# Attention in steps of four heads, with logits and value products in plain fp32 on halves of the array

## The chip, the core and the metric

The kernel runs on one core of a Trainium2 chip. The metric is the device time of one execution in microseconds (us). The engines are PE (TensorE, matmuls; PEld is its weight load), DVE (VectorE), ACT (ScalarE), POOL (GpSimd) and SP, which issues most DMAs.

## The reference

One layer of a decoder trunk on 256 positions of 1024 channels. Three attention branches stand beside each other: MoBA attention (A, 4 heads; with 256 positions one block, so plain causal attention with a position bias), forgetting attention (B, 4 heads, the bias is a running sum of log gates) and sliding-window attention with sinks (C, 8 query heads over 2 key heads). Heads have 64 channels. All is float32.

```python
z = rmsnorm(x, ln1) @ w_in            # q, k, v of A, B, C; forget gates; three merge gates
o_a = moba_attention(qa, ka, va, tbl_a)
o_b = forgetting_attention(qb, kb, vb, fb + b_f)
o_c = sliding_window_sink_attention(qc, kc, vc, sinks, tbl_c)
#   each: softmax(q k^T * SCALE + bias, causal or windowed) v
merged = sigmoid(ga) * (o_a @ w_pa) + sigmoid(gb) * (o_b @ w_pb) + sigmoid(gc) * (o_c @ w_pc)
x = x + merged @ w_o
u = causal_dwconv(rmsnorm(x, ln2) @ w_up, conv_w, conv_b)
a, b = split(u)
out = rmsnorm(x + (silu(a) * b) @ w_down, ln_f)
```

## The kernel before

All large products use fp32r, a one-pass format, three times: an operand is split into a high part (a copy by ACT into an fp32r tile, `hi`) and a low part (a subtraction by DVE, `lo`), and TensorE adds high x high, low x high and high x low (`mm3`, lines 254 to 258). The weights stream in by DMA as `raw` pieces of 128x1024; ACT makes `whi` of each (line 110) and DVE `wlo` (line 117), up to five pieces ahead of their matmuls.

The order of all instructions is written out by hand. A generator, `filler`, yields the projection matmuls one by one, each with an estimate of its time: q and k of B, v of B, q and k of A, v of A and C, q of C, k of C (line 407 and `mm3`), then six gate groups of 48 matmuls with 512 columns (`group_gates`). `now` is the sum of these estimates. Everything else is a task, a generator that does one stage, then yields a delay after which its next stage is put between the filler's matmuls. `AT` has the starting times of the tasks and `DL` the delays. Engines run their own instructions in the order written, so a stage that is not ready holds up what stands behind it.

Attention is eight tasks, `pair(p)`, p from 0 to 7, of two heads each: 0 and 1 are B, 2 and 3 are A, 4 to 7 are C. The two heads of a pair are in partitions 0 to 63 and 64 to 127 of q. The keys are stored twice, each with the other head's half set to zero by POOL, so that one matmul over all 128 rows gives both heads' logits side by side. Stages of a pair:

- logits (line 610): for each half of the 256 queries three fp32r matmuls, of 256 columns (keys 0 to 127 of both heads) into bank `s0` and of 512 (all keys) into `s1`;
- softmax: DVE adds the bias and takes the minimum of the negated logits (line 618), ACT takes the exponential and the sums (line 627), DVE scales by the reciprocal (line 640);
- six 128x128 transposes of the weights into banks `pt` and `o` (line 647), copied out by ACT, with a low part by DVE (lines 650 to 654);
- values (lines 660 and 663): six fp32r matmuls of 256 columns with zero-padded v, and two plain fp32 ones of 128 columns for the second half of the keys, into `pt`;
- the result's high and low part (lines 666 and 668) in `oT`, which the output projections read later.

PSUM has eight banks: four `acc` for the projections, and `s0`, `s1`, `pt`, `o` with one buffer each, so a new use of one of them waits until the last reader of the earlier one is done. Behind attention come the output projections, the merge, and the MLP, which the change doesn't touch.

Of the kernel before, what the change touches and what calls it, by code (L numbers as in the profile page):

```python
# [35 lines left out]
AT = dict(norm=1.59, positions=9.23, out0=26.0, out1=20.0, gates=18.2, sums=23.0, pairs=(37.46,  # L36
          44.7, 52.4, 61.33, 67.8, 74.76, 83.2, 90.9), mm=14.0)
DL = dict(pos=1.0, sq0=0.5, sq1=0.53, rs=1.0, row=1.0, q=1.98, qlo=1.17, v=0.83, vlo=0.8, g1=0.47,
          g2=0.64, s1=1.0, s2=1.43, s3=1.0, b=0.8, qk=1.9, ex=2.56, sc=1.21, fl=0.45, fl2=0.71,
          lo=0.8, va=0.91, vh=0.6)  # L40
# [100 lines left out]
def hybrid_kernel(ctx: ExitStack, tc: tile.TileContext, x, xT, ln_f, w_main, w_v1, w_v2, b_f, sinks,  # L141
# [88 lines left out]
    def q_tiles(n, name):  # L230
        return [at.tile([P, n, S], F32R, name=name + x) for x in "hl"]

    def k_tiles(n, name):

        ks = [at.tile([P, n, 2, S], F32R, name=name + x) for x in "hl"]
        for k in ks:
            nc.gpsimd.memset(k[0:64, :, 1, :].bitcast(F32), 0.0)
            nc.gpsimd.memset(k[64:128, :, 0, :].bitcast(F32), 0.0)
        return ks

    def v_tiles(n, name):

        vs = [at.tile([P, n, 2, P], F32 if x == "1" else F32R, name=name + x) for x in "hl1"]
        for v in vs:
            w = v if v is vs[2] else v.bitcast(F32)
            nc.gpsimd.memset(w[:, :, 0, 64:128], 0.0)
            nc.gpsimd.memset(w[:, :, 1, 0:64], 0.0)
        return vs

    qB, qA, qC = q_tiles(2, "qB"), q_tiles(2, "qA"), q_tiles(4, "qC")  # L250
    kB, vB, kA, vA = k_tiles(2, "kB"), v_tiles(2, "vB"), k_tiles(2, "kA"), v_tiles(2, "vA")
    kC, vC = k_tiles(1, "kC"), v_tiles(1, "vC")
# [172 lines left out]
    room = G[:, 0].rearrange("p t (n c) -> p (t n) c", c=512)  # L425
    turn = [0]

    def scaled(acc, width, scale):

        turn[0] += 1  # L430
        tmp = room[:, turn[0] % 4, :width].rearrange("p (b s) -> p b s", s=S)
        r = rs["row1"][:, None, :].to_broadcast([P, width // S, S])
        nc.vector.scalar_tensor_tensor(tmp, acc[:, :width].rearrange("p (b s) -> p b s", s=S),
                                       scale, r, op0=OP.mult, op1=OP.mult)
        return tmp

    def q_out(dst, b0, acc):
        bs = slice(b0, b0 + 2)
        tmp = scaled(acc, 512, SCALE)
        nc.scalar.activation(dst[0][:, bs], tmp, AF.Copy)  # L440
        return lambda: nc.vector.tensor_sub(dst[1][:, bs], tmp, dst[0][:, bs].bitcast(F32))

    def k_out(dst, acc, width):
        tmp = scaled(acc, width, 1.0)
        halves = list(enumerate((slice(0, 64), slice(64, 128))))
        for e, h in halves:
            nc.scalar.activation(dst[0][h, :, e, :], tmp[h], AF.Copy)

        def low():
            for e, h in halves:  # L450
                nc.vector.tensor_sub(dst[1][h, :, e, :], tmp[h], dst[0][h, :, e, :].bitcast(F32))
        return low

    def v_out(dst, acc, t):
        a = acc.rearrange("p (b e d) -> p b e d", e=2, d=HD)
        r = rs[1][:, t:t + 1]
        hs = [dst[2 if t else 0][:, :, e, e * 64:e * 64 + 64] for e in range(2)]
        for e in range(2):
            nc.scalar.activation(hs[e], a[:, :, e, :], AF.Identity, scale=r)

        def low():
            for e in range(2):
                lo = dst[1][:, :, e, e * 64:e * 64 + 64]
                nc.vector.scalar_tensor_tensor(lo, a[:, :, e, :], r, hs[e].bitcast(F32),
                                               op0=OP.mult, op1=OP.subtract)
        return low if t == 0 else None

    def group_qk(q, k, name, later=None):
        accs = [bank("acc", 512, 4) if later is None else bank(tag, 512) for tag in ("pt", "o")]
        for i in range(4):  # L470
            yield from qk_piece(accs, 2 * i, 2, 512)

        def out():
            assert "row1" in done
            low = q_out(q, 0, accs[0])
            yield DL["q"]
            low2 = q_out(q, 2, accs[1]) if k is None else k_out(k, accs[1], 512)
            low()
            yield DL["qlo"]
            low2()  # L480
            done.add(name)
        spawn(out(), 0.0 if later is None else later)

    def group_kc():
        acc = bank("acc", 512, 4)
        yield from qk_piece([acc], 0, 8, P)

        def out():
            low = k_out(kC, acc, S)
            yield DL["qlo"]  # L490
            low()
            done.add("kC")
        spawn(out())
# [3 lines left out]
    def group_v1():  # L497
# [9 lines left out]
        def out():  # L507
            low = v_out(vB, accs[0][:, 0:256], 0)
            v_out(vB, accs[1][:, 0:256], 1)
            yield DL["v"]  # L510
            low()
            done.add("vB")
        spawn(fox(logits), AT["gates"])
        spawn(out(), AT["out1"])

    def group_v2():
# [4 lines left out]
        def out():  # L521
            low = [v_out(vA, accs[0][:, 0:256], 0), v_out(vC, accs[0][:, 256:384], 0)]
            yield DL["v"]
            v_out(vA, accs[1][:, 0:256], 1)
            v_out(vC, accs[1][:, 256:384], 1)
            for f in low:
                f()
            done.add("vA")
        spawn(out())
# [74 lines left out]
    def pair(p):  # L604
        q, qi, k, ki, v, vi, bias, j = pair_of(p)
        assert done >= ({"B", "vB", "foxb"} if p < 2 else {"A", "vA"} if p < 4 else {"C", "kC"}), p
        s0, s1 = bank("s0", S), bank("s1", 512)
        for sc, qs, n in ((s0, slice(0, P), P), (s1, slice(P, S), S)):
            for i, (a, b) in enumerate(((0, 0), (1, 0), (0, 1))):
                nc.tensor.matmul(sc, q[a][:, qi, qs], k[b][:, ki, :, 0:n], start=i == 0,  # L610
                                 stop=i == 2)
        yield DL["qk"]
        L = at.tile([P, 2, ROWS], F32, name="L", tag="L", bufs=1)
        nm = small([2, 2], "nm")
        for e in range(2):
            least = 3.0e38 if j is None else skn[:, j + 4 * e:j + 4 * e + 1]
            for i, (sc, lo, n) in enumerate(((s0, 0, P), (s1, P, S))):
                nc.vector.tensor_tensor_reduce(
                    out=L[:, e, lo:lo + n], in0=sc[:, e * n:(e + 1) * n], in1=bias[e][i],
                    scale=-1.0, scalar=least, op0=OP.add, op1=OP.min, accum_out=nm[:, e, i:i + 1])  # L620
        sm, sd = small([2, 2], "sm"), small([2, 2], "sd")
        if j is not None:
            nc.vector.tensor_sub(sd, nm, skn[:, j:j + 5:4][:, :, None].to_broadcast([P, 2, 2]))
        for e in range(2):
            for i, (lo, n) in enumerate(((0, P), (P, S))):
                a = L[:, e, lo:lo + n]
                nc.scalar.activation(a, a, AF.Exp, scale=-1.0, bias=nm[:, e, i:i + 1],
                                     accum_out=sm[:, e, i:i + 1])
        if j is not None:
            nc.scalar.activation(sd, sd, AF.Exp)  # L630
        done.add(p)
        yield DL["ex"]
        if j is not None:
            nc.vector.tensor_add(sm, sm, sd)
        r = small([2, 2], "rs")
        nc.vector.reciprocal(r, sm)
        for e in range(2):
            for i, (lo, n) in enumerate(((0, P), (P, S))):
                a = L[:, e, lo:lo + n]
                nc.vector.tensor_scalar(a, a, r[:, e, i:i + 1], None, op0=OP.mult)  # L640
        yield DL["sc"]
        pTh, pTl, pT1 = [at.tile([P, 2, n], d, name="pT" + x, tag="pT" + x, bufs=1)
                         for x, n, d in (("h", S, F32R), ("l", S, F32R), ("1", P, F32))]
        pts = [bank(tag, ROWS) for tag in ("pt", "o")]
        for e in range(2):
            for i in range(3):
                nc.tensor.transpose(pts[e][:, i * P:(i + 1) * P], L[:, e, i * P:(i + 1) * P], ident)  # L647
            yield DL["fl"] if e else DL["fl2"]
        for e in range(2):
            nc.scalar.activation(pTh[:, e, :], pts[e][:, 0:S], AF.Copy)  # L650
            nc.scalar.activation(pT1[:, e, :], pts[e][:, S:ROWS], AF.Copy)
        yield DL["lo"]
        for e in range(2):
            nc.vector.tensor_sub(pTl[:, e, :], pts[e][:, 0:S], pTh[:, e, :].bitcast(F32))
# [431 lines left out]
```

## Time and profile before

| | |
|---|---|
| median of 3 runs | 392.74 us (392.5 to 393.16) |
| the profiled execution | 392.43 us, span of its instructions 390.7 us |
| busy: PE, DVE, ACT, POOL | 97%, 77%, 61%, 4% of the span |
| PE's granted clock | 0.996 on the mean of the span |

A matmul's record is longer than the time that it adds, since matmuls are pipelined; the chain of work that ended last shows the time that each adds. A plain fp32 matmul leaves two records, an fp32r matmul or a transpose one. A form such as 34*12 behind a name is the part of the array that a matmul uses, rows by columns.

### The profile page before, as it was taken

The page shows a single profiled execution, that of the slowest core. Times are in us where ns is not written, and L with a number is a line of the kernel's source. Part 1 is how long each engine was busy: PE and PEld are TensorE (multiplying, and loading weights), DVE is VectorE, ACT ScalarE, POOL GpSimd, SP SyncE. Part 2 cuts the span into 40 slices and gives each one's busy share as a digit, 9 for nine tenths or more (in the row PEclk, how much of TensorE's full clock was granted, in tenths as well). Part 3 has the DMA queues.
Part 4 walks back from the last instruction along what each step waited for, and adds up shares of the span by engine and source line. Part 5 has one row for each costly group of instructions (what it writes and reads, how often), then busy time and mean ns, then how long its engine had stood idle before and what let it go on. Part 6 is the DMA issues. An engine that isn't in the chain of part 4 may idle for free.

```text
span 390.7 us, 6636 instructions
## 1 busy us (share of the span) xinstructions
PE 379.8 (97%) x2464; PEld 345.7 (88%) x2464; DVE 301.6 (77%) x572; ACT 239.5 (61%) x431; POOL 15.7 (4%) x50
## 2 busy tenths in 40 slices
PE   5999999999999999999999999999999999999992
PEld 5999999888888888888899999999999999999982
DVE  3877998775876727967779999878887888888745
ACT  4875767647566587326587767655665556655533
POOL 4711000000000000000000000000000000000000
PEclk9999999999999999999999999999999999999998
DMA  7989775442533446443736567656465655463002
GB/s 188 393 315 331 281 213 179 153 132 103 187 125 117 164 141 235 161 163 107 269 109 216 168 227 251 209 182 204 164 208 180 206 167 201 173 216 108 2 1 108
DMA packets 21376, 70.88 MB, mean 181 GB/s; under 512 B 2504, under 2 KB 3413, under 8 KB 21344
## 3 DMA queue, kind: packets, MB, share of 16 engines
q1 hardware_dynamic: 20448, 68.05, 51.8%
q0 software_dynamic: 752, 2.18, 1.8%
q8 instruction: 19, 0.31, 0.3%
q10 hardware_dynamic: 144, 0.23, 0.2%
q14 instruction: 13, 0.11, 0.1%
HBM read 69.38 MB, written 1.07 MB: 180 GB/s over the span
## 4 chain that ended last, share of the span: by engine, by line
PE 96%; DMA 1%; DVE 1%; SPq 0%; ACT 0%; issue 0%; DVEq 0%
PE s L874 16%; PE acc L256 15%; PE acc L258 15%; PE acc L257 15%; PE pt L874 8%; PE o L874 8%; PE acc L407 7%; PE s L610 2%; PE pt L660 1%; DMA raw<-in_w_main 1%; PE pt L407 1%; PE o L407 1%; PE pt L663 1%; PE o L647 1%; PE pt L647 1%; PE s L314 0%
## 5 line engine op out<-in xcount | busy, mean ns | idle before, releaser
L117 DVE TENSOR_TENSOR wlo<-raw,whi 128x1024 fp32r<-128x1024 f32 (+4 forms) x131 | 150.5, 1162 | 15.4 <-ACT whi L110 15.2
L110 ACT ACTIVATE whi<-raw 128x1024 fp32r<-128x1024 f32 (+4 forms) x131 | 129.0, 1006 | 34.9 <-PE acc L257 21.0
L256 PE MATMUL acc<-whi,hThi 128*128 128x512 f32 (+2 forms) x160 | 62.3, 390 | 0.0
L258 PE MATMUL acc<-wlo,hThi 128*128 128x512 f32 (+2 forms) x160 | 60.1, 376 | 0.0
L257 PE MATMUL acc<-whi,hTlo 128*128 128x512 f32 (+2 forms) x160 | 59.9, 374 | 0.0
L874 PE MATMUL s<-oThi,whi 128*128 128x256 f32 x176 | 49.3, 281 | 0.0
L874 PE MATMUL s<-oThi,wlo 128*128 128x256 f32 x176 | 49.2, 280 | 0.0
L874 PE MATMUL s<-oTlo,whi 128*128 128x256 f32 x176 | 48.9, 280 | 0.0
L882 ACT ACTIVATE ya<-v,cv 128x256 f32<-128x256 f32 x22 | 13.3, 603 | 42.7 <-DVE v L879 42.7
L258 PEld LDWEIGHTS acc<-wlo,hThi 128*128 128x128 f32 x160 | 30.0, 188 | 5.3
L257 PEld LDWEIGHTS acc<-whi,hTlo 128*128 128x128 f32 x160 | 30.2, 189 | 4.5 <-DVE hTlo L308 0.2
L256 PEld LDWEIGHTS acc<-whi,hThi 128*128 128x128 f32 x160 | 30.1, 188 | 4.3
L257 PE MATMUL acc<-whi,al 128*128 128x512 f32 (+1 forms) x88 | 33.8, 384 | 0.0
L258 PE MATMUL acc<-wlo,ah 128*128 128x512 f32 (+1 forms) x88 | 33.8, 384 | 0.0
L256 PE MATMUL acc<-whi,ah 128*128 128x512 f32 (+1 forms) x88 | 33.8, 384 | 0.0
L874 PEld LDWEIGHTS s<-oTlo,whi 128*128 128x128 f32 x176 | 33.5, 191 | 0.0
L874 PEld LDWEIGHTS s<-oThi,whi 128*128 128x128 f32 x176 | 33.0, 188 | 0.4
L874 PEld LDWEIGHTS s<-oThi,wlo 128*128 128x128 f32 x176 | 33.0, 188 | 0.4
L874 PE MATMUL pt<-oThi,whi 128*128 128x256 f32 x88 | 24.8, 282 | 0.0
L874 PE MATMUL pt<-oThi,wlo 128*128 128x256 f32 x88 | 24.7, 281 | 0.0
L874 PE MATMUL pt<-oTlo,whi 128*128 128x256 f32 x88 | 24.7, 281 | 0.0
L874 PE MATMUL o<-oThi,whi 128*128 128x256 f32 x88 | 24.7, 281 | 0.0
(301 smaller groups left out, 802.1 us busy)
## 6 DMA issues: line engine op xcount, KB each, us to landing
raw<-in_w_main SPq DMA_DIRECT2D x115, 512.0 KB, 3.3
raw<-in_w_main SPq DMA_DIRECT2D x7, 256.0 KB, 5.9
raw<-in_w_v SPq DMA_DIRECT2D x4, 384.0 KB, 4.2
xt<-in_x SPq DMA_DIRECT2D x2, 512.0 KB, 6.9
G<-rowsd POOLq DMA_DIRECT2D x1, 1024.0 KB, 13.7
raw<-in_w_v SPq DMA_DIRECT2D x2, 390.0 KB, 6.3
G<-in_xT SPq DMA_DIRECT2D x3, 256.0 KB, 6.3
out_y<-xt SPq DMA_DIRECT2D x2, 288.0 KB, 2.2
```

The source lines that it names most:

```text
L110: self.nc.scalar.activation(self.parts[i][0][:, cs], self.raw[i][:, cs], AF.Copy)
L117: self.nc.vector.tensor_sub(lo[:, cs], self.raw[i][:, cs], hi[:, cs].bitcast(F32))
L256: nc.tensor.matmul(o, lh, rh, start=start, stop=False, **kw)
L257: nc.tensor.matmul(o, ll, rh, start=False, stop=False, **kw)
L258: nc.tensor.matmul(o, lh, rl, start=False, stop=stop, **kw)
L407: nc.tensor.matmul(o, w[:, kk, cs], hT[h][:, k, :], start=first, stop=last, skip_group_check=True)
L610: nc.tensor.matmul(sc, q[a][:, qi, qs], k[b][:, ki, :, 0:n], start=i == 0, stop=i == 2)
L647: nc.tensor.transpose(pts[e][:, i * P:(i + 1) * P], L[:, e, i * P:(i + 1) * P], ident)
L660: nc.tensor.matmul(o, v[a][:, vi, e, :], b[:, e, :], start=e == 0 and n == 0, stop=False, **kw)
L663: nc.tensor.matmul(o[:, P:S], v[2][:, vi, e, :], pT1[:, e, :], start=False, stop=e == 1, **kw)
L874: nc.tensor.matmul(u, w, h2T[h][:, k, :], start=k == 0 and i == 0, stop=k == KD - 1 and i == 2)
L882: nc.scalar.activation(y, v, AF.Identity, scale=w[2], bias=w[3])
```

## The change

`four(n)`, n from 0 to 3, takes the place of `pair(p)` and handles pairs 2n and 2n+1 in each stage. q, k and v are kept in float32 as they come, with no high and low part, no second copy and no zeros; ACT or DVE writes each once. The logits of a head are plain fp32 matmuls on its 64 partitions, so each head of a pair uses its own half of the array's rows; they go into one bank per head. The values of a head are plain fp32 matmuls with 64 columns of v as weights, each head of a pair in its own half of the array's columns, into the two halves of one bank. The transposed weights are copied out once, in float32. The tables of times and delays are new.

```diff
-          s3=1.0, b=0.8, qk=1.9, ...
+AT = dict(norm=1.59, positions=9.23, out0=26.0, out1=20.0, gates=18.2, sums=23.0,
+          fours=(37.46, 53.0, 68.5, 83.5), mm=14.0)
+DL = dict(pos=1.0, sq0=0.5, sq1=0.53, rs=1.0, row=1.0, q=1.98, g1=0.47, g2=0.64, s1=1.0, s2=1.43,
+          s3=1.0, b=0.8, qk=1.9, half=2.0, ex=2.6, sc=1.3, fl=1.2, va=1.9, vh=0.9)
...
+    def qk_tiles(n, name):
+        return at.tile([P, n, S], F32, name=name)
     def v_tiles(n, name):
+        return [at.tile([P, n, 2, HD], F32, name=name + x) for x in "01"]
...
+    def scaled(dst, acc, scale):
+        n = dst.shape[1]
+        r = rs["row1"][:, None, :].to_broadcast([P, n, S])
+        nc.vector.scalar_tensor_tensor(dst, acc[:, :n * S].rearrange("p (b s) -> p b s", s=S),
                                        scale, r, op0=OP.mult, op1=OP.mult)
...
     def v_out(dst, acc, t):
         a = acc.rearrange("p (b e d) -> p b e d", e=2, d=HD)
         r = rs[1][:, t:t + 1]
+        nc.scalar.activation(dst[t], a, AF.Identity, scale=r)
...
+    def four(n):
+        need = ({"B", "vB", "foxb"}, {"A", "vA"}, {"C", "kC"}, {"C", "kC"})[n]
+        assert done >= need, n
+        pairs = [pair_of(2 * n + i) for i in range(2)]
+        sc = [bank(tag, ROWS) for tag in ("s0", "s1", "pt", "o")]
+        for i, (q, qi, k, ki, *_) in enumerate(pairs):
+            for lo, qs, m in ((0, slice(0, P), P), (P, slice(P, S), S)):
+                for e in range(2):
+                    h = slice(e * HD, (e + 1) * HD)
+                    nc.tensor.matmul(sc[2 * i + e][:, lo:lo + m], q[h, qi, qs], k[h, ki, 0:m],
+                                     start=True, stop=True)
         yield DL["qk"]
...
+            yield DL["ex"] if i else DL["half"]
...
+        pT = at.tile([P, 4, ROWS], F32, name="pT", tag="pT", bufs=1)
+        pts = [bank(tag, ROWS) for tag in ("s0", "s1", "pt", "o")]
+        for h in range(4):
             for i in range(3):
+                nc.tensor.transpose(pts[h][:, i * P:(i + 1) * P], L[:, h, i * P:(i + 1) * P], ident)
+        yield DL["fl"]
+        for h in range(4):
+            nc.scalar.activation(pT[:, h, :], pts[h], AF.Copy)
         yield DL["va"]
         kw = dict(skip_group_check=True)
+        os = [bank(tag, S) for tag in ("s0", "s1")]
+        for i, (*_, v, vi, _, _) in enumerate(pairs):
+            for t, cs in ((0, slice(0, S)), (1, slice(P, S))):
+                for e in range(2):
+                    p = pT[:, 2 * i + e]
+                    nc.tensor.matmul(os[i][e * HD:(e + 1) * HD, cs], v[t][:, vi, e, :],
+                                     p[:, S:ROWS] if t else p[:, 0:S], start=t == 0, stop=t == 1,
+                                     **kw)
         yield DL["vh"]
+        for i in range(2):
+            nc.scalar.activation(oT[0][:, 2 * n + i, :], os[i], AF.Copy)
         yield DL["vh"]
+        for i in range(2):
+            nc.vector.tensor_sub(oT[1][:, 2 * n + i, :], os[i],
+                                 oT[0][:, 2 * n + i, :].bitcast(F32))
```

The order on TensorE at the first logits. Before, pair 0 has six fp32r matmuls over the whole array (`kBh`, `kBl`, `qBh`, `qBl` are the high and low parts):

```order
L610 MATMUL s_791<-kBh,qBh 128x256 [waits DVE_49,Activation_49,Pool_49]
L610 MATMUL s_791<-kBh,qBl 128x256
L610 MATMUL s_791<-kBl,qBh 128x256 [waits Pool_49]
L610 MATMUL s_792<-kBh,qBh 128x512 [waits DVE_49]
L610 MATMUL s_792<-kBh,qBl 128x512
L610 MATMUL s_792<-kBl,qBh 128x512
```

Now, at the same place, the first step has eight matmuls, the two heads of a pair in turn (s0 and pt are the heads on rows 0 to 63, s1 and o those on rows 64 to 127):

```order
L566 MATMUL s0_728<-kB_143,qB_140 128x128 [waits DVE_49]
L566 MATMUL s1_729<-kB_143,qB_140 128x128 [waits DVE_49]
L566 MATMUL s0_728<-kB_143,qB_140 128x256
L566 MATMUL s1_729<-kB_143,qB_140 128x256
L566 MATMUL pt_730<-kB_143,qB_140 128x128
L566 MATMUL o_731<-kB_143,qB_140 128x128
L566 MATMUL pt_730<-kB_143,qB_140 128x256
L566 MATMUL o_731<-kB_143,qB_140 128x256
```

All four heads of B now have their logits here; before, pair 1 followed 72 matmuls later.

The order on TensorE around the values of A's last heads. Before, three gate matmuls out of nine that follow are shown, and the wait of what comes next is one for the softmax's result:

```order
L660 MATMUL pt<-pTl,vAh 128x256
L660 MATMUL pt<-pTl,vAh 128x256 [waits DVE_49]
L663 MATMUL pt<-pT_1248,vA_169 128x128
L663 MATMUL pt<-pT_1248,vA_169 128x128 [waits Activation_49]
L256 MATMUL acc<-whi,hThi 128x512
L257 MATMUL acc<-whi,hTlo 128x512
L258 MATMUL acc<-wlo,hThi 128x512
```

Now the values of the second step are followed by three gate matmuls and then by the logits of the third:

```order
L619 MATMUL s_1133<-pT,vA_148 64x256 [waits PE_49,Activation_49]
L619 MATMUL s_1133<-pT,vA_148 64x256 [waits Activation_49]
L619 MATMUL s_1133<-pT,vA_149 64x128 x2
L243 MATMUL acc<-whi,hThi 128x512
L244 MATMUL acc<-whi,hTlo 128x512
L245 MATMUL acc<-wlo,hThi 128x512
L566 MATMUL s_1155<-kC,qC 128x128 [waits DVE_49]
L566 MATMUL s_1156<-kC,qC 128x128 [waits DVE_49]
L566 MATMUL s_1155<-kC,qC 128x256
L566 MATMUL s_1156<-kC,qC 128x256
```

The logits moved up to the values whose two banks they use again: they wait for DVE's subtractions of these values.

On DVE at the same place, now (`G<-acc` is the eviction of the second gate group, `oTlo` the low part of the values):

```order
L646 TENSOR_SCALAR G<-acc,nq 128x512 [waits PE_49]
L116 TENSOR_TENSOR wlo<-raw,whi 128x1024 [waits DMAHW5_49,Activation_49]
L627 TENSOR_TENSOR oTlo<-s_1132,oThi 128x256 [waits Activation_49]
L627 TENSOR_TENSOR oTlo<-s_1133,oThi 128x256 [waits Activation_49]
L578 ISA L,nm<-s_1155,G,skn 128x128 [waits DVE_49,DMASW7_49,PE_49,Pool_49]
```

The two subtractions stand behind an eviction and a weight remainder; before, a single one stood at a pair's end and freed `pt` alone.

In the last two steps the logits of the fourth stand directly ahead of the values of the third, which take banks s0 and s1 next:

```order
L566 MATMUL pt<-kC,qC 128x256
L566 MATMUL o<-kC,qC 128x256
L619 MATMUL s_1344<-pT,vC_150 64x256 [waits DVE_49]
L619 MATMUL s_1344<-pT,vC_150 64x256
L619 MATMUL s_1344<-pT,vC_151 64x128 x2
```

Before, no pair's logits stood directly ahead of another's values: at least 6 projection matmuls lay between them.

## Rows read from the trace of the kernel before

**Rows 1.** The page: span, TensorE's busy time, granted clock, chain that ended last.

```profile
span 390.7 us, 6636 instructions
...
PE 379.8 (97%) x2464; PEld 345.7 (88%) x2464; DVE 301.6 (77%) x572; ACT 239.5 (61%) x431; POOL 15.7 (4%) x50
...
PEclk9999999999999999999999999999999999999998
...
PE 96%; DMA 1%; DVE 1%; SPq 0%; ACT 0%; issue 0%; DVEq 0%
```

**Rows 2.** Busy time by stretch: length, then engines, granted clock, DMA share, GB/s.

```profile
50.00:150.00 100.00, 100.00 (x563) 86.50 (x562) 70.89 (x181) 66.97 (x156) 0.56 (x1) 1.00 0.46 150
```

**Rows 3.** Chain of work, pair 0 and pair 1: start, time on the path, what.

```profile
51.76 0.12 PE acc L407
51.88 1.06 PE s L610 x6
...
59.41 0.33 PE pt L647 x3
...
60.57 0.33 PE o L647 x3
...
61.50 1.05 PE s L610 x6
...
64.58 0.72 PE pt L660 x6
65.30 0.45 PE pt L663 x4
```

**Rows 4.** Chain of work around the 34-row matmul, line 381.

```profile
17.48 0.72 PE o L407 x6
18.20 0.74 PE s L381 x2
18.94 0.91 PE pt L407 x6
```

**Rows 5.** Chain of work around the four 8-row matmuls, line 576.

```profile
40.85 0.17 PE acc L257
...
41.20 0.65 PE s L576 x4
41.85 0.37 PE acc L256
```

**Rows 6.** Chain of work around the two transposes into 8 partitions, line 568.

```profile
38.19 0.22 PE s L568 x2
38.41 0.71 PE acc L407 x6
```

**Rows 7.** Chain of work: plain fp32, two of 128 columns; one of 4.

```profile
24.50 0.45 PE s L302 x4
...
34.76 0.22 PE s L557 x2
```

**Rows 8.** Lines by form, ACT and DVE, 50 to 150 us: busy us, mean ns.

```profile
L110 ACT ACTIVATE whi<-raw 128x1024 fp32r<-128x1024 f32 x28 | 29.4, 1058 | 14.8 <-PE acc L257 12.3 <-issue 1.1 <-ACT kCh L447 0.8
L666 ACT ACTIVATE oThi<-pt 128x256 fp32r<-128x256 f32 x8 | 3.0, 381 | 3.7 <-PE pt L663 3.7
...
L117 DVE TENSOR_TENSOR wlo<-raw,whi 128x1024 fp32r<-128x1024 f32 x30 | 36.2, 1220 | 8.9 <-ACT whi L110 8.8
L668 DVE TENSOR_TENSOR oTlo<-pt,oThi 128x256 fp32r<-128x256 f32 x8 | 3.4, 423 | 7.2 <-ACT oThi L666 7.2
L686 DVE TENSOR_SCALAR G<-acc,nq 128x512 f32<-128x512 f32 x4 | 3.0, 752 | 6.4 <-PE acc L258 6.4
```

**Rows 9.** Timeline of DVE: the reductions of two heads of C.

```profile
96.92 0.35 DVE L618 CUSTOM_DVE_ANT_0 L<-s,G,skn 128x128 f32<-128x128 f32 x1 [0.29 <-issue]
...
97.60 0.35 DVE L618 CUSTOM_DVE_ANT_0 L<-s,G,skn 128x128 f32<-128x128 f32 x1
```

**Rows 10.** Timeline of PE: start, length. Then the chain's time for 512 columns.

```profile
56.85 0.28 PE L407 MATMUL acc<-hTlo,whi 128*128 128x256 f32 x1
...
56.97 0.28 PE L407 MATMUL acc<-hThi,wlo 128*128 128x256 f32 x1
...
101.61 0.23 PE acc L257
```

More of the change, by code (lines that the diff above doesn't have):

```diff
@@ L228, in hybrid_kernel @@
     at = attn_ctx.enter_context(tc.tile_pool(name="attn", bufs=1))
[L230 to L239, printed above, removed]
-    def v_tiles(n, name):
[L243 to L252, printed above, removed]
+    def qk_tiles(n, name):
+        return at.tile([P, n, S], F32, name=name)
+    def v_tiles(n, name):
+        return [at.tile([P, n, 2, HD], F32, name=name + x) for x in "01"]
+    qB, qA, qC = qk_tiles(2, "qB"), qk_tiles(2, "qA"), qk_tiles(4, "qC")
+    kB, kA, kC = qk_tiles(2, "kB"), qk_tiles(2, "kA"), qk_tiles(1, "kC")
+    vB, vA, vC = v_tiles(2, "vB"), v_tiles(2, "vA"), v_tiles(1, "vC")
     def mm3(o, lhs, rhs, start, stop, **kw):
@@ L474, in out @@
             assert "row1" in done
-            low = q_out(q, 0, accs[0])
+            scaled(q[:, 0:2], accs[0], SCALE)
             yield DL["q"]
[L477 to L480, printed above, removed]
+            if k is None:
+                scaled(q[:, 2:4], accs[1], SCALE)
+            else:
+                scaled(k, accs[1], 1.0)
             done.add(name)
@@ L507, in out @@
         def out():
[L508 to L511, printed above, removed]
+            for t in range(2):
+                v_out(vB, accs[t][:, 0:256], t)
             done.add("vB")
+            yield 0.0
         spawn(fox(logits), AT["gates"])
@@ L521, in out @@
         def out():
[L522 to L527, printed above, removed]
+            for t in range(2):
+                v_out(vA, accs[t][:, 0:256], t)
+                v_out(vC, accs[t][:, 256:384], t)
             done.add("vA")
+            yield 0.0
         spawn(out())
@@ L602, in pair_of @@
         return qC, j, kC, 0, vC, 0, bias, j
[L604 to L611, printed above, removed]
-        yield DL["qk"]
[L613 to L645, printed above, removed]
-            for i in range(3):
[L647 to L654, printed above, removed]
@@ new lines, in four @@
+    def four(n):
[9 more added lines that the diff above has]
+                                     start=True, stop=True)
+        yield DL["qk"]
+        L = at.tile([P, 4, ROWS], F32, name="L", tag="L", bufs=1)
+        nm, sm, sd, r = (small([4, 2], x) for x in ("nm", "sm", "sd", "rs"))
+        for i in range(2):
+            bias, j = pairs[i][6:]
+            hs = slice(2 * i, 2 * i + 2)
+            for e in range(2):
+                least = 3.0e38 if j is None else skn[:, j + 4 * e:j + 4 * e + 1]
+                h = 2 * i + e
+                for t, (lo, m) in enumerate(((0, P), (P, S))):
+                    nc.vector.tensor_tensor_reduce(
+                        out=L[:, h, lo:lo + m], in0=sc[h][:, lo:lo + m], in1=bias[e][t],
+                        scale=-1.0, scalar=least, op0=OP.add, op1=OP.min,
+                        accum_out=nm[:, h, t:t + 1])
+            if j is not None:
+                nc.vector.tensor_sub(sd[:, hs], nm[:, hs],
+                                     skn[:, j:j + 5:4][:, :, None].to_broadcast([P, 2, 2]))
+            for h in (2 * i, 2 * i + 1):
+                for t, (lo, m) in enumerate(((0, P), (P, S))):
+                    a = L[:, h, lo:lo + m]
+                    nc.scalar.activation(a, a, AF.Exp, scale=-1.0, bias=nm[:, h, t:t + 1],
+                                         accum_out=sm[:, h, t:t + 1])
+            if j is not None:
+                nc.scalar.activation(sd[:, hs], sd[:, hs], AF.Exp)
+            yield DL["ex"] if i else DL["half"]
+        done.update((2 * n, 2 * n + 1))
+        for i in range(2):
+            hs = slice(2 * i, 2 * i + 2)
+            if pairs[i][7] is not None:
+                nc.vector.tensor_add(sm[:, hs], sm[:, hs], sd[:, hs])
+            nc.vector.reciprocal(r[:, hs], sm[:, hs])
+            for h in (2 * i, 2 * i + 1):
+                for t, (lo, m) in enumerate(((0, P), (P, S))):
+                    a = L[:, h, lo:lo + m]
+                    nc.vector.tensor_scalar(a, a, r[:, h, t:t + 1], None, op0=OP.mult)
+            yield DL["sc"]
+        pT = at.tile([P, 4, ROWS], F32, name="pT", tag="pT", bufs=1)
+        pts = [bank(tag, ROWS) for tag in ("s0", "s1", "pt", "o")]
+        for h in range(4):
+            for i in range(3):
+                nc.tensor.transpose(pts[h][:, i * P:(i + 1) * P], L[:, h, i * P:(i + 1) * P], ident)
+        yield DL["fl"]
+        for h in range(4):
+            nc.scalar.activation(pT[:, h, :], pts[h], AF.Copy)
@@ L655, in pair @@
         yield DL["va"]
-        o = bank("pt", S)
         kw = dict(skip_group_check=True)
-        for n, (a, b) in enumerate(((0, pTh), (1, pTh), (0, pTl))):
-            for e in range(2):
-                nc.tensor.matmul(o, v[a][:, vi, e, :], b[:, e, :], start=e == 0 and n == 0,
-                                 stop=False, **kw)
-        for e in range(2):
-            nc.tensor.matmul(o[:, P:S], v[2][:, vi, e, :], pT1[:, e, :], start=False, stop=e == 1,
-                             **kw)
+        os = [bank(tag, S) for tag in ("s0", "s1")]
@@ L667, in pair @@
         yield DL["vh"]
-        nc.vector.tensor_sub(oT[1][:, p, :], o, oT[0][:, p, :].bitcast(F32))
+        for i in range(2):
+            nc.vector.tensor_sub(oT[1][:, 2 * n + i, :], os[i],
+                                 oT[0][:, 2 * n + i, :].bitcast(F32))
     def group_gates(br, half):
@@ L717, in hybrid_kernel @@
     spawn(positions(), AT["positions"])
-    for p, u in enumerate(AT["pairs"]):
-        spawn(pair(p), u)
+    for n, u in enumerate(AT["fours"]):
+        spawn(four(n), u)
     for cost in filler():
```

44 lines of the change are left out of this document (4 added, 40 removed).

## The prediction

> **What bounds the kernel now.** I read the page first. TensorE is busy for 97% of the 390.7 us span at the full granted clock (2.4 GHz), and the chain that ended last is 96% PE [rows 1]. Attention runs between 50 and 150 us, so the stretch is what matters: there PE is busy 100 of 100 us, DVE 70.89, ACT 66.97, and DMA at 0.46 [rows 2]. Busy TensorE alone proves little, since a matmul's record is 0.28 us long while the next starts 0.12 us later [rows 10]. So I read the chain of work in order of time, which gives each matmul's own share of the path: pieces follow each other without a gap, 0.12 us for a 256-column and 0.23 us for a 512-column fp32r matmul [rows 3, 10]. Nothing on DVE, ACT or POOL ends a wait of TensorE here. What counts is the number of TensorE slots in the eight pairs, and any wait that the new order puts between them.
>
> **What a pair costs on TensorE.** Logits: six fp32r matmuls, 1.05 us. Transposes: twice three, 0.33 us each time, 0.11 us apiece. Values: six fp32r matmuls, 0.71 us, and two plain fp32 ones (four records), 0.45 us [rows 3]. Two pairs, which is one of the new steps of four heads: logits 2.10, transposes 1.32, values 2.32 us. There are four such steps.
>
> **What leaves at no gain.** The low parts of q, k, v and of the transposed softmax weights, and the zero halves, are work of DVE, ACT and POOL, and none of it ends a TensorE wait; it lies under a TensorE that is busy throughout [rows 2]. Costed at nothing; the cover is the gate matmuls, and nothing is exposed by taking covered work away. Transposes are unchanged in number: nothing.
>
> **What TensorE does instead.** Per step of four heads, the logits are eight plain fp32 matmuls on half the rows (four of 128 columns, four of 256), the values eight on half the columns, of the same sizes. A plain fp32 matmul has two records, and of 128 columns it takes half of 0.45 us: 0.11 us a record, call it u [rows 7]. The 384-column one bears this out as linear: 0.74 us, of which 0.10 is the switch below, is 0.64, or six records' worth of u [rows 4]. So a 256-column one is 4u, a 128-column one 2u.
> - One after another, a block of eight is 4 x 2u + 4 x 4u = 24u = 2.64 us. That is the upper bound; all rows of plain fp32 here are of this kind.
> - If the two heads of a pair run fully beside each other, it is 12u = 1.32 us, the lower bound.
> - In between: matmuls start in the order written, and each has two records on its own half. First head first record, first head second record, second head first record: the third may run beside the second, but not beside the first. Laying out the sixteen records so (each starts when its half is free and the one before it has started), both blocks end at 15u = 1.65 us. No row shows two halves at once. I take this value since the rows show an array that takes the next matmul long before the last one has left (0.12 against 0.28 us [rows 10]), and two halves share neither rows nor, in the logits, a bank.
> - Weight loads: three fp32 matmuls with 4 columns still take about 0.11 us a record [rows 7], so a full-width load alone holds the path for u. The logits block has 16 of these loads; if they queue, it takes 16u = 1.76 us rather than 1.65. The values' loads are half as wide and fit. I take 1.76 and 1.65.
>
> **Switching the array's division.** The kernel before already does this three times. Around the four matmuls on 8 rows: they take 0.65 where four take 0.48 (+0.17), and the first 384-column matmul after them takes 0.37 instead of 0.17 (+0.20), so in and out cost 0.37 [rows 5]. Around the 34-row matmul: 0.10 going in and 0.91 instead of 0.72 for the six after it, 0.29 together [rows 4]. But the two transposes into 8 output partitions, a split by columns alone, take 0.22 for two and 0.71 for the six after: no cost [rows 6]. So a logits block (split by rows) pays 0.37; a values block (by columns) pays between 0 and 0.37, and I take 0.20. The Trainium skill (TensorEngine Tiling (Array Packing), Key Properties) says that a change of tiling mode, not just of tile, drains TensorE, which speaks against this change; rows 4 and 5 agree, rows 6 do not show it. By that rule every block pays 0.37, and the sum would be 4 x 0.17 = 0.7 us higher. In the last two steps the logits of one stand directly ahead of the values of the other, which saves one switch, 0.2 us in all.
>
> **The waits that the new order adds.** Banks s0, s1, pt and o now serve logits, transposes and values in turn, so a step can block the next.
> - At the end of the second gate group (call it time 0) the order is: values of the second step, three gate matmuls, logits of the third, which wait for the values' banks. TensorE gets there at 1.85 + 0.70 = 2.55 us. ACT has a weight conversion first (1.06), then the two copies of the values (0.38 each): done near 1.5 and 1.9. DVE has the gate group's eviction (0.75) and a weight remainder (1.22) first, until 2.1, then the two subtractions (0.42 each): 2.5 and 2.9 [rows 8]. The second logits matmul needs s1 at about 2.65: some 0.3 us of wait, with all later gate matmuls queued behind it.
> - The values of the third step stand right behind the logits of the fourth and need s0 and s1 back from DVE's reductions, two for a head in 0.68 us (from 96.92 to 97.60 [rows 9]). The first head's logits end about 1.1 us into the block, so s0 is free near 1.9, when TensorE is done with the logits (1.96): at most 0.1 us.
> - Transposes come 85 small or 54 large matmuls after their logits (10 us or more), and values 15 large ones (3.5 us) after the transposes, against four copies of some 0.5 us and a conversion (1.06): no wait, with about 0.4 us to spare. If ACT is late by more than that, this is the next wait.
> Together 0.4 us; the ends are 0 and about 3.
>
> **The sum.** Per step: logits 1.76 + 0.37 - 2.10 = +0.03; values 1.65 + 0.20 - 2.32 = -0.47. Four steps: -1.76. Shared switch -0.2, waits +0.4: **-1.55 us**. The profiled execution took 392.43 us (span 390.7, 1.73 around it), 0.31 below the median of the runs shown, 392.74; I put the difference on the median: **391.2 us**. With the column switch at its ends (-0.8 to +0.7) and the waits from 0 to 1.4, this case alone gives 390.0 to 392.9.
>
> **The rivals.**
> - *No overlap.* Each half waits for the other, 24u a block: logits +0.91, values 2.64 + 0.20 - 2.32 = +0.52, four times 1.43 = 5.7, less 0.2, plus 0.4: +5.9, **398.6 us**. For it: every fp32 row here is serial, and 256 columns of plain fp32 are 0.44 us against 0.12 of one fp32r pass, so without overlap two heads cost more than three padded passes. Against it: only the depth of the pipeline. It decides as soon as a block takes more than about 20u: then logits and values together lose what they now gain.
> - *Full overlap.* 12u a block, loads too: logits -0.41, values -0.80, four times -1.21 = -4.84, less 0.2, plus 0.8 since DVE then returns the banks later than TensorE wants them: -4.2, **388.5 us**. Nothing in the trace decides it; against it speaks that each matmul's two records follow each other on one half. The Trainium skill (TensorE: Matmul & The Clock Gate, Part 3) has matmuls in different tiles start about 4 ns apart and run concurrently; by that rule this is the case that comes, and no row here shows it.
> - *One split overlaps, the other not.* Logits alone: (0.03 + 0.52) x 4 + 0.2 = +2.4; values alone: (0.91 - 0.47) x 4 + 0.2 = +2.0. About **394.9 us**. The two splits are different: by rows two banks are written, by columns one bank, and both heads then read all 128 rows.
> - *The banks come back late.* If DVE or ACT is one more weight conversion behind at two or three of the places above, the waits are 3 us instead of 0.4: **393.8 us**. It decides from 2 us of waits on. For it: four tasks now share four banks; against it: DVE and ACT have 30 us of every 100 free [rows 2] and lose work.
>
> **Chances.** Forecast 0.38, full overlap 0.18, no overlap 0.27, one split only 0.12, late banks 0.05. A measurement of this kernel can tell about 0.2%, 0.8 us. The forecast's own range (390.0 to 392.9) lies seven parts in ten below 391.95, the rest within; full overlap is faster; the other three are slower. Faster 0.45, same 0.11, slower 0.44. Both signs hold much, so the range must reach from full overlap into the case without it: 388.4 to 399.0; less than 2 in 10 lies outside.
>
> **What would show it.** In the chain of work after: logits blocks of 8 matmuls near 1.8 us (1.3 with full overlap, 2.6 without), values blocks near 1.65; 0.2 us extra on the first matmul behind each; TensorE idle or stretched by 0.3 us ahead of the third step's logits; all else as before, DVE and ACT less busy. The forecast is wrong if a block takes 20u or more, or if a TensorE wait for DVE or ACT of over 1 us stands before a logits or values block.

## The result, and the profile after

The changed kernel takes **387.99 us** (median of 4 runs, 387.09 to 388.68). The kernel before took 392.95 us beside it (392.5 to 393.94, 4 runs). The ratio is 0.9875, with a 95% interval of 0.9857 to 0.9893: 1.25% or 5.0 us faster. 391.2 us was forecast: the direction was right, the gain was three times as large, and the time is what the rival *full overlap* gave (388.5).

The page of the changed kernel, the lines that answer to [rows 1]:

```profile
span 387.0 us, 6530 instructions
...
PE 377.2 (97%) x2464; PEld 340.1 (88%) x2464; DVE 287.7 (74%) x540; ACT 230.7 (60%) x399; POOL 8.0 (2%) x20
...
PEclk9899999999999999999999999999999999999998
...
PE 96%; DMA 1%; DVE 1%; SPq 0%; ACT 0%; issue 0%; DVEq 0%
```

Its busy time by stretch, the columns as in [rows 2]:

```profile
50.00:150.00 100.00, 99.81 (x588) 82.62 (x587) 61.62 (x156) 65.23 (x139) 0.56 (x1) 1.00 0.47 156
5.00:10.00 5.00, 3.03 (x17) 2.62 (x17) 2.09 (x6) 2.63 (x6) 0.37 (x1) 0.95 0.98 276
10.00:15.00 5.00, 5.00 (x33) 5.00 (x33) 4.77 (x11) 4.28 (x9) 0.58 (x1) 0.71 1.05 407
```

TensorE still bounds attention. DVE has lost 9 of 71 us there and ACT 2 of 67, and TensorE now stands still for 0.2 us. The two lower lines are the start-up of this one execution: the granted clock is 0.71 on the mean of 10 to 15 us, a mix of the two levels 1.2 and 2.4 GHz, after a stretch in which TensorE was busy 3.03 of 5 us (the profiled execution before was busy 2.41 there and kept 1.00). Some executions of nearly every kernel here have a lower mean clock and take some 1.3 us longer, so medians hold a mix, and differences below 1 us are read from the traces.

The chain of work, first and second step, answers to [rows 3] (start, time on the path, what; L566 logits, L619 values, L394 and L243 projections):

```profile
53.12 0.86 PE s L566 x8
53.98 0.10 PE pt L566
54.08 0.01 PE o L566
...
54.62 0.01 PE o L566
```

```profile
70.36 1.45 PE s L619 x16
71.81 0.43 PE acc L243
```

The logits block is done at 54.63: 1.51 us for four heads, where two pairs took 2.10 before. The values block takes 1.45, where two pairs took 2.32. The first matmul behind a block takes 0.43 where the next ones take 0.23, so leaving the halves costs 0.20. With u = 0.109 us (a record of 128 columns of plain fp32, the prediction's 0.11) 12u is 1.31: the logits block is 12u and 0.20 for the switch, the values block 12u and 0.14.

The timeline of TensorE in the second half of that logits block (start, length; `pt` is the head on rows 0 to 63, `o` that on rows 64 to 127) shows where the time went:

```profile
53.81 0.27 PE L566 MATMUL pt<-kB,qB 64*128 64x128 f32 x1
53.82 0.27 PE L566 MATMUL o<-kB,qB 64*128 64x128 f32 x1
53.92 0.27 PE L566 MATMUL pt<-kB,qB 64*128 64x128 f32 x1
53.93 0.27 PE L566 MATMUL o<-kB,qB 64*128 64x128 f32 x1
```

Each head's records of 128 columns follow each other at u, and those of the other head start 0.01 us behind. The Trainium skill (TensorE: Matmul & The Clock Gate, Part 3) has matmuls in different tiles start about 4 ns apart; this trace agrees, with 0.01 us.

The chain at the third step's logits, and where the fourth's logits meet the third's values:

```profile
95.81 1.00 PE s L566 x5
...
97.25 0.43 PE o L566 x2
97.68 0.43 PE acc L243
```

```profile
114.88 0.91 PE s L566 x8
115.79 0.33 DVE L L578
...
116.13 0.40 DVE L L578
...
116.59 1.55 PE s L619 x16
118.14 0.43 PE acc L243
```

The third block takes 1.87 instead of 1.51: 0.36 us for bank `s1`, which DVE's subtraction returns late. At the fourth, logits and values begin 1.71 us apart, 0.2 of which is a wait for DVE's reductions, and the values take 1.55, 0.10 more than where they follow without a wait: 0.30 in all. These are the only two waits of TensorE, 0.66 us together.

The bookkeeping of attention, in the two profiled executions: before, from the first logits at 51.88 to the end of the last values at 143.58, 91.70 us; after, 53.12 to 136.81, 83.69 us. 15 gate matmuls fewer lie between (3.45 us), so attention itself saves 4.56. The blocks give 4 x (1.51 + 0.20 - 2.10) + 4 x (1.45 + 0.20 - 2.32) = -4.24, the shared switch -0.2, the waits +0.66: -3.8. The other 0.8 lie in the projection matmuls between; there are 11 interruptions now and 32 before. By the starts of their records, gate matmuls follow each other at 0.227 us where nothing has come between for long, and some 0.005 wider in the first ten behind an interruption; from 75 us on this adds up to 0.5 us before and 0.15 now. It accounts for about half of the 0.8; the rest stays open.

### The profile page after: what moved, and what is told of

Read it like the earlier page. It is cut to its first block, busy times and chain, and to the rows that moved or that the text cites. A ratio compares the mean times of both kernels' runs of the same rounds, so it can differ in the third digit from the quotient of the medians.

```text
span 387.0 us, 6530 instructions
## 1 busy us (share of the span) xinstructions
PE 377.2 (97%) x2464; PEld 340.1 (88%) x2464; DVE 287.7 (74%) x540; ACT 230.7 (60%) x399; POOL 8.0 (2%) x20
## 4 chain that ended last, share of the span: by engine, by line
PE 96%; DMA 1%; DVE 1%; SPq 0%; ACT 0%; issue 0%; DVEq 0%
PE s L834 16%; PE acc L243 16%; PE acc L244 15%; PE acc L245 15%; PE pt L834 8%; PE o L834 8%; PE acc L394 7%; PE pt L394 2%; PE s L619 2%; PE o L394 1%; DMA raw<-in_w_main 1%; PE s L566 1%; PE s L608 1%; PE s L301 0%; PE pt L566 0%; PE pt L773 0%
## 5 line engine op out<-in xcount | busy, mean ns | idle before, releaser
L243 PE MATMUL acc<-whi,hThi 128*128 128x512 f32 (+2 forms) x160 | 61.3, 383 | 0.0
L243 PEld LDWEIGHTS acc<-whi,hThi 128*128 128x128 f32 x160 | 30.1, 188 | 6.0 <-issue 1.3
L243 PE MATMUL acc<-whi,ah 128*128 128x512 f32 (+1 forms) x88 | 33.8, 384 | 0.0
```

The source lines that it names most:

```text
L243: nc.tensor.matmul(o, lh, rh, start=start, stop=False, **kw)
```

## The experiments

After the result this was to be told apart: whether the halves overlap wherever their matmuls stand, or only where neighbours in the order are on different halves; what the steps of four heads are worth beside the halves; and whether the relief of DVE, ACT and POOL has a share in the gain.

**Halves apart.** All matmuls of one half first, then those of the other, in the logits:

```diff
-        for i, (q, qi, k, ki, *_) in enumerate(pairs):
-            for lo, qs, m in ((0, slice(0, P), P), (P, slice(P, S), S)):
-                for e in range(2):
+        for e in range(2):
+            for i, (q, qi, k, ki, *_) in enumerate(pairs):
+                for lo, qs, m in ((0, slice(0, P), P), (P, slice(P, S), S)):
```

> The changed kernel with the logits of a step written head by head over both pairs: all four matmuls on rows 0 to 63 first, then all four on rows 64 to 127. Same work, same switches. Theory (the two halves run beside each other because matmuls of the two heads stand next to each other in the order written): a logits block grows from 12 to about 24 units of 0.11 us, from 1.5 to 2.8 us in the chain, four times 1.3 = 5.3 us more: about 393.3 us. Rival 1 (the array takes any matmul whose half is free, in whatever order): no change, 388.0. Rival 2 (the gain of the change does not come from halves at all but from less work on DVE, ACT and POOL): no change either.

389.88 us (389.46 to 391.59), ratio 0.9928 [0.9904, 0.9952]. Neither number came. The chain of work at the first block:

```profile
51.51 0.85 PE s L566 x4
...
53.12 0.66 PE o L566 x4
53.78 0.43 PE acc L394 x2
```

and its timeline where the second half begins (`pt` is the fifth record of the first half, `s` is bank `s1`, the first record of the second; PEld is its weight load):

```profile
52.20 0.27 PE L566 MATMUL pt<-kB,qB 64*128 64x128 f32 x1
52.20 0.18 PEld L566 LDWEIGHTS s<-kB,qB 64*128 64x128 f32 x1
52.20 0.37 PE L566 MATMUL s<-kB,qB 64*128 64x128 f32 x1
52.31 0.27 PE L566 MATMUL pt<-kB,qB 64*128 64x128 f32 x1
...
52.42 0.27 PE L566 MATMUL s<-kB,qB 64*128 64x128 f32 x1
```

2.27 us: 0.20 and 19u, where wholly one after another would be 24u. The second half starts 7u after the first, while its own first matmul stands eight records behind; three records ahead of it in the order start later than it does. So a half is not bound to the order written, but it does not see past every matmul ahead of it. Four blocks longer by 0.76 are 3.0 us, and the two waits (0.66) have gone: +2.4. Attention (51.51 to 137.62) is 86.11 us against 83.69, +2.4. At the fourth step no wait stands between logits and values any more, and the values are back at 1.45:

```profile
116.84 0.66 PE o L566 x4
117.50 1.45 PE s L619 x16
```

The same edit in the values:

> The changed kernel with the values of a step written head by head: all four matmuls on columns 0 to 63 first, then all four on columns 64 to 127. Theory: a values block grows from 1.45 to about 2.8 us in the chain, four times 1.3 = 5.3 us more: about 393.3 us. Rivals as for the logits: no change, 388.0. If only one of the two splits overlaps by neighbourhood, this and the run with the logits apart differ.

390.83 us (389.54 to 391.6), ratio 0.9946 [0.9921, 0.9972]. The chain of work has the block at 2.15 instead of 1.45:

```profile
69.89 2.15 PE s L619 x16
72.04 0.43 PE acc L243
```

Four times 0.70 is the 2.8 us by which the medians differ; attention (52.65 to 138.94) is 86.29 us, +2.6, since the third step's wait for banks shrinks. The column split behaves as the row split does.

**Heads in turn per pair.** In each pair both matmuls of one head, then both of the other:

```diff
-            for lo, qs, m in ((0, slice(0, P), P), (P, slice(P, S), S)):
-                for e in range(2):
+            for e in range(2):
+                for lo, qs, m in ((0, slice(0, P), P), (P, slice(P, S), S)):
```

> The changed kernel with the two inner loops of the logits swapped: per pair both matmuls of the first head, then both of the second. Theory (neighbours only, starts in order): of each pair 256 columns of the first head can run beside 128 of the second and little else, 16 to 20 units a block instead of 12, 0.4 to 0.9 us a step: 389.8 to 391.5 us. Rival (the array looks further ahead than the next matmul): 388.0. Were starts strictly in order and records not interleaved, 18 units or 390.6.

387.84 us (387.35 to 388.48), ratio 0.9879 [0.9854, 0.9904]: no difference that can be measured. In the chain the block is 51.34 to 52.95, 1.61 us, one u longer. So the halves need not alternate strictly, and the theory that only neighbours overlap falls.

**Further ahead.** Three matmuls of one half, three of the other, then the last of each:

```diff
-        for i, (q, qi, k, ki, *_) in enumerate(pairs):
...
+        first, last = [(0, 0), (0, 1), (1, 0)], [(1, 1)]
+        for e, some in ((0, first), (1, first), (0, last), (1, last)):
+            for i, t in some:
```

> Only the order of the eight logits matmuls of a step is changed: three of the one half of the rows (two of 128 columns, one of 256), three of the other half, then the last of 256 columns of each. Theory: a half may start a matmul up to four records (two plain fp32 matmuls) ahead of its turn, as the run with the halves apart showed; three matmuls of the busy half hold the other one back until the first of them is done, 2u, so a block is 14u plus the switch, 1.74 us in place of 1.51, and the kernel 388.0 + 4 x 0.23 = 388.9 us less what the waits absorb, 388.5 to 388.9. Rival 1, look-ahead without a limit: 1.51 us, 388.0 us. Rival 2, strictly in the order written: the second half starts when the third matmul of the first is under way, 8u later; 20u or more, 2.4 us and 390.5 us or more.

389.33 us (387.47 to 390.66), ratio 0.9914 [0.9887, 0.9942]. The runs spread too far to tell 0.5 us; the trace tells it. The chain of work, first block:

```profile
51.33 0.96 PE s L567 x6
...
52.73 0.43 PE o L567 x2
53.17 0.55 PE acc L394 x3
```

1.84 us: 0.20 and 15u, against 14u expected by the look-ahead of four records. Both rivals (1.51 and 2.4) are out, and the third and fourth step's waits take up their share, so attention (51.33 to 135.70) is 84.37 against 83.69 us. Taken together, blocks take 12u, 13u, 15u and 19u with two, four, six and eight records of one half ahead of the other's. One rule fits the runs beyond two: the first record of the other half, and its weight load, start with the record four places ahead, at most 0.01 us behind it. It was 52.04 and 52.03 in the second pair of the heads in turn, 51.59 for both here, 52.20 for both with the logits apart and 70.52 for both with the values apart. That first record takes 0.21 us, 2u: its load begins with it and lies under no earlier matmul of its half. This is the one u that the expected 14u lacked. In the values, whose weights have 64 columns, the first record takes 0.27 where the next of its size takes 0.22, half the excess.

**Two heads at a time.** The new arithmetic in steps of one pair, at the eight starting times of the kernel before (its stages and their delays are rewritten for a pair too):

```diff
-          fours=(37.46, 53.0, 68.5, 83.5), mm=14.0)
+          pairs=(37.46, 44.7, 52.4, 61.33, 67.8, 74.76, 83.2, 90.9), mm=14.0)
...
-    def four(n):
+    def pair(p):
...
-        sc = [bank(tag, ROWS) for tag in ("s0", "s1", "pt", "o")]
+        sc = [bank(tag, ROWS) for tag in ("s0", "s1")]
```

> The new arithmetic (plain fp32, halves of the array, no low parts) in steps of two heads at the starting times of the kernel before: eight logits blocks and eight values blocks, 6 units each. Theory (each block pays 0.34 to 0.4 us for going into and out of the split array): logits 0.66 + 0.40 against 1.05 before, values 0.66 + 0.34 against 1.16: -0.16 a pair, -1.3 us on the kernel before, about 391.5; so four heads at a time are worth some 3.5 us. Rival (the switches hide behind other work, and the four-head step is only a matter of form): about 388.

391.15 us (390.79 to 392.73), ratio 0.9967 [0.995, 0.9984], as expected. The chain of work, logits of the first two pairs:

```profile
51.50 0.86 PE s L564 x8
52.36 6.67 PE acc L394 x54
```

A pair's block is 0.86, half of 1.31 and 0.20. By the ratios, halves alone bring 0.33% (1.3 us) of the 1.25%, and the steps of four the other 0.92% (3.6 us). The traces give much the same: attention (51.50 to 141.61) is 90.11 us. It has three gate matmuls fewer than before (0.69), so halves alone save 0.9 there; it has twelve more than the changed kernel (2.76), so the steps of four save 3.7. Eight blocks fewer at 0.34 to 0.40 of switches are about 3.0 us of that, and the shared one 0.2 more. The waits nearly cancel: 0.66 in the changed kernel, and here 0.5 at transposes whose scaled weights DVE returns late, behind a weight remainder:

```profile
112.60 0.30 DVE L L594
...
113.03 0.61 PE pt L600 x3
```

**The removed work put back as idle work.** First most of it (POOL fills; low parts of q and k; a subtraction behind each copy of the transposed weights; v's low parts are left out). DVE is then busy for 297.7 us and ACT for 234.3; they had 301.6 and 239.5 before, and 287.7 and 230.7 in the changed kernel. All of it goes into tiles that nothing reads:

```diff
+    for _ in range(8):
+        nc.gpsimd.memset(idle[0][0:64, 0:512], 0.0)
...
+    def low_part(src, w):
+        nc.scalar.activation(idle_r[:, 0:w], src, AF.Copy)
+        nc.vector.tensor_sub(idle[2][:, 0:w], src, idle_r[:, 0:w].bitcast(F32))
...
             nc.scalar.activation(pT[:, h, :], pts[h], AF.Copy)
+            nc.vector.tensor_sub(idle[1][:, 0:S], pts[h][:, 0:S], pT[:, h, 0:S])
```

> The changed kernel with the work that the change removed put back as idle work: 30 POOL fills of the zeros' sizes, a copy by ACT and a subtraction by DVE for q, k (low parts), and one DVE subtraction of 128x256 per head behind each copy of the transposed weights. Its results go to tiles that nothing reads; all of the computation stays. Theory: the whole gain is TensorE's (blocks of 1.5 us in place of 2.1 and 2.3), and work of DVE, ACT and POOL costs nothing as long as it lies under a busy TensorE: 388.0 us, within 0.8 us of the changed kernel, blocks still 1.5 us. Rival: part of the gain is the relief of DVE and ACT, which return banks and weights sooner: 389.5 to 392 us, and the chain of work shows new waits of TensorE for DVE or ACT of 1 us or more in all.

390.37 us (389.15 to 391.0), ratio 0.9936 [0.9914, 0.9958]: the rival's number. Blocks are still 1.5 us, so the theory's first half stands and its second falls. Then the two parts by themselves:

> Of the idle work of the earlier run (390.4 us) only the POOL fills and the copies and subtractions for q and k are kept; the subtraction behind each copy of the transposed weights is left out. Results go to tiles that nothing reads. Theory: only DVE work that stands ahead of a bank's return in the new order costs time, and this part does not: 388.0 us, within 0.8. Rival: DVE and ACT work costs wherever it stands, in proportion: half of the 2.4 us and more, 389.2 us or above.

388.03 us (387.36 to 389.35), ratio 0.9875 [0.9851, 0.9898]: it costs nothing that can be measured.

> The other part alone: one DVE subtraction of 128x256 behind each copy of the transposed weights, its result unused, all else as in the changed kernel. Theory: DVE stands still behind ACT's copies and comes late to a weight remainder and the reductions of the fourth step and to the subtractions that free banks for the third; TensorE waits there 0.3 and 0.9 us longer: 389.4 us, up to 390.4. Rival: 388.0 us, since it is work of DVE under a busy TensorE.

388.76 us (388.54 to 390.15), ratio 0.9893 [0.987, 0.9917]; by median 0.8 us more than the changed kernel, at both ends of the range 1.5. The chain of work with the subtractions alone, behind the fourth step's logits:

```profile
112.02 1.15 ACT pT L612 x3
...
113.17 0.44 DVE idlea L613
...
114.07 1.22 DVE wlo L116
...
116.01 1.55 PE s L621 x16
117.56 0.43 PE acc L244
```

The chain has left TensorE. DVE stands behind ACT's copies with the idle subtraction, then does a weight remainder, and only then the reductions that give back `s0` and `s1`; the values start 2.62 us after the logits (113.39 in the timeline) instead of 1.78 (114.81 to 116.59). At the third step's logits the same lateness costs 0.6 more. Where DVE's work stands decides, not how much there is. The two places together are the 1.4 us that the trace shows: from the first record of the first logits to that of the last values it is 83.63 us (51.08 to 134.71), against 82.24 (53.05 to 135.29) in the changed kernel. With all idle work it is 83.63 too (52.66 to 136.29), so the subtractions are the whole of its delay in attention. The medians, 0.8 and 2.4 us above the changed kernel, lie on either side of 1.4; what the 2.4 holds beyond it is not settled.

**Other starting times.** The third step 1.4 and the fourth 3.3 later in the table, to be rid of the two waits:

```diff
-          fours=(37.46, 53.0, 68.5, 83.5), mm=14.0)
+          fours=(37.46, 53.0, 69.9, 86.8), mm=14.0)
```

> Only two starting times of the table are changed: the third step of four heads starts at 69.9 instead of 68.5 and the fourth at 86.8 instead of 83.5, so that nine projection matmuls instead of three (third step) stand between the values of one step and the logits of the next, and at the fourth too instead of none. Theory: the two waits of TensorE, 0.36 us for the third step's banks and 0.2 us for the fourth's, are gone, and the switch that the fourth's logits shared with the third's values is paid again, +0.2: 388.0 - 0.35 = 387.6 us. Rival: the waits move to the next place where a bank or a softmax result is late, and the time stays at 388.0 or rises by the 0.2.

393.29 us (391.72 to 393.7), ratio 1.001 [0.9995, 1.0025]: the whole gain lost. Both waits are gone, but the chain of work at the fourth step shows a new one:

```profile
133.47 0.33 PE o L608 x3
...
135.10 3.88 ACT G L650 x4
138.99 0.95 ACT whi L109
139.93 0.39 ACT pT L611
...
140.36 3.11 PE s L619 x13
```

The transposes now come behind the moment at which ACT turns to the gates: the copies of the transposed weights stand behind four passes of 128x1024 (3.88 us) and a weight conversion. TensorE is idle for 3.14 us, and behind that the granted clock is low, as the busy time by stretch shows (0.50, that is 1.2 GHz):

```profile
140.00:142.00 2.00, 1.64 (x9) 1.40 (x11) 1.19 (x1) 2.00 (x5) 0.00 (x0) 0.50 0.03 8
```

The values take 3.11 us there, and 1.45 elsewhere. The expectation's rival ("the waits move to the next place") was right in kind and far too small.

With the fourth step at 85.4, six projection matmuls earlier, the copies stand ahead of the gates again:

> As the run with shifted starts, but the fourth step starts at 85.4 instead of 86.8, six projection matmuls earlier, so that ACT copies its transposed weights ahead of the table load and the four passes over the gates, and not behind them. Theory: the 3.1 us wait and the 1.7 us at a lowered clock behind it are gone; third step's wait for banks (0.36) and fourth's (0.2) are gone too, the shared switch costs 0.2, and the fourth's logits stand three matmuls behind the third's values and may wait up to 0.4 us for banks: 387.6 to 388.0 us. Rival: the two waits of the changed kernel come back elsewhere: 388.3 us or more.

387.3 us (387.23 to 388.3), ratio 0.9856 [0.9831, 0.9881]. The chain of work, third and fourth logits:

```profile
95.66 0.86 PE s L566 x8
...
97.16 0.01 PE o L566
```

```profile
116.71 0.96 PE s L566 x6
...
118.22 0.12 PE o L566
118.34 0.43 PE acc L243
```

1.51 us, and 1.63 with 0.12 of wait for a bank; no other wait of TensorE. From the first logits to the last values, with nine gate matmuls more in between (2.05), it is 85.44 us: 0.3 less than the changed kernel, as two waits of 0.66 gone, 0.12 of a new one and the shared switch paid again give. It has the lowest median of all, but 0.3 us is less than these runs can tell from the changed kernel.

## Why the prediction was off, step by step

- **What bounds the kernel** [rows 1, 2]: right. TensorE's slots decide, and the chain after is PE to 96% as well.
- **Staggered halves: this step failed.** The prediction put a block at 15u = 1.65 us since "matmuls start in the order written, and each has two records on its own half", and at 1.76 for the logits because 16 full-width loads were taken to queue. The trace shows 12u = 1.31 for both. Records of the other half start 0.01 us after those of the first, ahead of their turn, and in the runs out of turn they pass up to three records. So "Engines run their own instructions in the order written", as the kernel is described above, does not hold on TensorE between two halves. In the timeline the weight loads of the two halves lie side by side too. [Rows 7] had loads only one after another on the whole array; to carry this over to two halves was the mistake. With the switch, a step's logits cost 1.71 instead of 2.13: four times 0.42, 1.7 us of the 3.4 that were missed.
- **The switch of the array.** Logits: 0.37 taken, 0.40 measured, right. Values: 0.20 taken, 0.34 measured. [Rows 6] misled: two transposes of 0.22 us show no switch, a block of values does, 0.14 in the block and 0.20 on the matmul behind it. The Trainium skill (TensorEngine Tiling (Array Packing), Key Properties), by which every change of mode drains TensorE, agrees with both splits here. This error hid part of the other one: values with the switch cost 1.65, forecast 1.85, four times 0.20.
- **One shared switch, -0.2**: as forecast; the fourth step's pair of blocks has one exit.
- **Waits +0.4**: 0.66, at the two places named and for the causes named (0.36 for `s1`, forecast 0.3; 0.30 for the reductions, forecast up to 0.1).
- **Low parts and zeros at no gain**: right for the order before, as far as the run in steps of two heads tells (0.9 to 1.3 us faster, where TensorE's slots alone gave 1.3), and not the whole truth for the new one. With the subtractions left in, the new order loses 0.8 us by the medians and 1.4 by the trace, since they put DVE's queue in front of bank returns. The low parts of q and k and POOL's fills are worth nothing.
- **The sum.** -1.55 - 1.7 - 0.8 + 0.26 = -3.8; the profile has -4.56 in attention, the medians -5.0. The 0.8 between the first two is in the projection matmuls, and no term of the prediction stood for it.
- **The rivals.** Full overlap was the true case, with 0.18 of the chance. That its 388.5 came within 0.5 us is in part luck: it had 0.20 for the values' switch (0.34) and 0.8 for waits (0.66), and with the measured terms its sum of -4.2 would be -3.8; the 0.8 in the projection matmuls made up for it. No overlap and one split only did not come. A late stage of the kind in *the banks come back late* came in one run only, with 3.1 us of idle TensorE, when the fourth step was moved by 3.3.

## What to carry to other kernels

Matmuls on two halves of the array, by rows or by columns, cost half, loads and double records included, if they are written in turn. For plain fp32 matmuls of 128 and 256 columns, as here, two of one half in a row cost 1u of 12u, three cost 3u, and four cost 7u, more than half of the overlap. Each block on halves pays about 0.35 to 0.40 us to enter and leave, so gather as many as the banks allow. Before a step is moved in a table of times, look at what stands ahead of its copies on ACT and DVE: 3.3 in the table cost 5 us.

## What was not expected of the hardware

- The other half of the array starts a matmul with the record four places ahead of it, so ahead of three earlier records that still wait for the busy half; with eight records ahead it starts only 7u (0.76 us) in. Its first record then shows its weight load (0.21 instead of 0.11 us).
- Weight loads of the two halves run at the same time: 16 full-width loads did not hold up a block of 1.31 us.
- Behind an idle stretch of 3.1 us in mid-kernel the granted clock was 0.50 over the next 2 us, so that the wait cost half as much again (3.11 instead of 1.45 us for the values).
